# A 1-core streaming block: a written order for the recurrence on three engines, and five Strassen stages instead of two in the second down projection

## The chip, the cores and the metric

The kernel runs on one core of one Trainium2 chip. The metric is the device time of one execution in microseconds (us). Smaller is better. Five engines work beside each other and wait for one another through semaphores: TensorE (PE in the profile; its weight loads are PEld), VectorE (DVE), ScalarE (ACT), GpSimd (POOL) and SyncE (SP), which here issues the DMA transfers.

## What is computed

One block of a streaming encoder on 512 tokens of width 1024: a half-step SwiGLU FFN, a token mixer, and a second half-step FFN. Each is modulated (shift, scale, gate from the conditioning vector c). The mixer joins a gated DeltaNet group (4 heads, causal convolution, chunked delta rule) and a latent-attention group (4 heads). Cut to what matters:

```python
def _swiglu(h, w_in, w_out):
    gate, up = jnp.split(h @ w_in, 2, axis=-1)
    return (jax.nn.silu(gate) * up) @ w_out

    # chunked delta rule, one step of the scan over chunks
    def step(state, inp):
        u_c, wk_c, qd_c, kd_c, qk_c, gl_c = inp
        v_new = u_c - jnp.einsum('bhck,bhkv->bhcv', wk_c, state)
        o_c = jnp.einsum('bhck,bhkv->bhcv', qd_c, state) + jnp.einsum('bhcs,bhsv->bhcv', qk_c, v_new)
        state = state * gl_c[..., None, None] + jnp.einsum('bhck,bhcv->bhkv', kd_c, v_new)
        return state, o_c

    o_a = _rms(o_a, gdn_norm_w) * jax.nn.silu(gz.reshape(B, S, GDN_HEADS, GDN_DV))
    mixed = jnp.concatenate([o_a.reshape(B, S, GDN_WIDTH), o_b.reshape(B, S, MLA_WIDTH)], axis=-1)
    return mixed @ w_out

        x = x + 0.5 * g1[:, None, :] * _swiglu(h, ffn1_w_in[l], ffn1_w_out[l])
        x = x + g2[:, None, :] * y      # y: the mixer of the modulated x
        x = x + 0.5 * g3[:, None, :] * _swiglu(h, ffn2_w_in[l], ffn2_w_out[l])
```

The hidden width of the FFNs is 2816, which is 22 tiles of 128. All values are fp32.

## The kernel before

**Products.** The transposed activations stay on chip, 512 tokens wide (`xT`, one tile for each 128 of the 1024 channels). Every fp32 value is split in a rounded part and a rest (`wh` and `wl` of a weight `wr`, `ah` and `al` of the hidden activations, `mh` and `ml` of the mixed heads), and a product is the sum of three matmuls (`mm3`: wh·xh, wh·xl, wl·xh, lines 468 to 470). A "dense product" below is one such matmul of 128 by 128 weights on 512 columns. ScalarE makes the rounded part by a cast, VectorE the rest by a subtraction, for weights in `split_w` (lines 228 and 229) or `sevenths` (line 269 on VectorE).

**Strassen stages.** In the gate/up products and in a part of the down projections a block of two output tiles, 8 tiles of the contraction and two halves of the tokens is treated as a 2 by 2 block product and computed by seven products, each 12 matmuls of 256 columns (L354 and, in the second down projection, L1250). The seven weight combinations (`sevenths`) and the activation combinations (`act_sums`, tiles `t`, split in `th` and `tl`) are made by VectorE and ScalarE beside TensorE. `seven_down` runs one such stage; `PAIRED = (4, 6)` names the first output tile of each.

**The second down projection** (`last_down`). There are 22 tiles of the contraction, in three parts (`KPARTS`: 8, 8 and 6 tiles). Output tiles 0 to 3 are dense, all 22. For tiles 4 and 5, and for 6 and 7, the first 8 contraction tiles are a Strassen stage, the other 14 are dense. The last tile's dense part is computed in two token halves. After each output tile VectorE adds it into `xT` (`update`, L1129), and `store` transposes it on TensorE (four times 128 by 128, L1286), copies it on ScalarE (L1288) and sends 256 KB through SyncE (L136). The end of the program is the last half tile: two updates, two transposes (L1228), a copy on ScalarE and one on VectorE, and two small stores.

**The recurrence** (`recur`, `gated_out`). The 512 tokens are four blocks `p` of 128. For each block, the matmuls with the state `S` (L1966, L1974) give `vn` on VectorE (L1968), which the matmuls for the new state (L1981) and for the output (L1989) read. The output `o` of a block is then normed (`gated_out`: squares on ScalarE, their sum `gs`, `ve`, an rsqrt `ry` on GpSimd at L214, the scaled `on` at L1475), transposed on TensorE (L2012), multiplied (`mf`), and split in `mh` and `ml`. Between these small steps TensorE fills with dense products of the output projection (`out_attended`, `out_half`, `out_rest`).

**What sets the order.** A scheduler of the tile framework orders each engine's instructions by a priority list and its own cost model. The context `matmuls_in_order` around the recurrence loop takes only TensorE out of its hands: the matmuls follow each other as the code writes them, save for the `loosely` recorded ones. VectorE and ScalarE are ordered by the scheduler there. Every engine works its queue in order; SyncE's queue holds all DMA transfers. Weight buffers (`wr`, `wh`, `wl`) come four at a time, accumulators (`pa`) three.

Of the kernel before, what the change touches and what calls it, by code (L numbers as in the profile page):

```python
# [19 lines left out]
P = 128  # L20
# [11 lines left out]
PAIRED = (4, 6)  # L32
# [64 lines left out]
class Block:  # L97
# [66 lines left out]
    @contextmanager  # L164
    def matmuls_in_order(self, after=None):

        self.loose = set()
        with self.traced() as block:
            yield
        for i in block:  # L170
            if i.engine == mybir.EngineType.PE and i.name not in self.loose:
                if after:
                    self.follow(i, after)
                after = i.name
        self.last_mm = after
# [81 lines left out]
    def unit_rows(self, w, t):  # L257

        raws = [self.raw_tile() for _ in range(2)]
        for i, raw in enumerate(raws):  # L260
            self.load(raw, w[:8 * P, (t + i) * P:(t + i + 1) * P].rearrange("(k p) f -> p k f", p=P))
        return lambda: self.sevenths(*raws, tile=lambda n: self.slot(F32R, n).rearrange("p (k f) -> p k f", k=4))
# [157 lines left out]
    def plan_units(self):  # L420
# [4 lines left out]
        def ffn(w1, w2, first, ts, seven=(), paired=()):  # L425
# [6 lines left out]
            for t in ts:  # L432
                if t in paired:
                    self.specs.append(lambda t=t: self.unit_rows(w2, t))
                for k0, n in KPARTS[1 if t in paired or t - 1 in paired else 0:]:
                    self.specs.append(lambda k0=k0, n=n, t=t: self.unit(w2[k0 * P:(k0 + n) * P, t * P:(t + 1) * P], n))

        ffn(ins["ffn1_w_in"][0], ins["ffn1_w_out"][0], 3, range(KT), SEVEN[0])
# [11 lines left out]
        ffn(ins["ffn2_w_in"][0], ins["ffn2_w_out"][0], 0, range(KT), SEVEN[1], PAIRED)  # L450
# [649 lines left out]
    def act_sums(self, whole):  # L1100

        l, r = slice(0, HALF), slice(HALF, NT)
        sub = lambda out, x, y: self.nc.vector.tensor_tensor(out=out, in0=x, in1=y, op=ALU.subtract)
        self.t7 = {1: [], 2: [], 3: [], 4: []}
        for a, b in zip(whole[:4], whole[4:]):
# [13 lines left out]
    def last_down(self, act, gate):  # L1119

        nc = self.nc
        full, l, r = slice(0, NT), slice(0, HALF), slice(HALF, NT)
        last, held = KT - 1, []
        side, sums, parts7 = Side(), Side(), Side()
# [7 lines left out]
        def run(p, u, ts, part, first=0, k=0, n=None):  # L1132
            k0, m = KPARTS[part]
            for j in range(k, k + (n or m)):
                xh, xl = act[k0 + j]
                self.mm3(p[:, ts], u[0][:, j, :], u[1][:, j, :], xh[:, ts], xl[:, ts], k0 + j == first, k0 + j == FT - 1)

        p = self.acc()
        for i, (k0, n) in enumerate(KPARTS):
            u = self.next_unit()  # L1140
            for k in range(0, n, 2):
                while any(not isinstance(a, tuple) for a in act[:k0 + k + 5]):
                    self.splits.step()
                run(p, u, full, i, 0, k, 2)
        held.append((0, full, p))
        p = self.acc()
        for i in range(3):
            run(p, self.next_unit(), full, i)
            side.step(4)
        held.append((1, full, p))  # L1150

        def ahead():
            parts7.add(self.raws.pop(0)())
            parts7.step(2)

        p = self.acc()
        for i in range(3):
            u = self.next_unit()
            for k in range(0, KPARTS[i][1], 2):
                run(p, u, full, i, 0, k, 2)  # L1160
                sums.step(2)
            if i == 0:
                side.flush()
                for h in held:
                    update(*h)
            elif i == 1:
                self.store(0, range(NB))
        sums.flush()
        update(2, full, p)
        p = self.acc()  # L1170
        for i in range(3):
            u = self.next_unit(ahead=1 if i < 2 else 0)
            if i == 0:
                self.preload(2)
            elif i == 1:
                ahead()
            for k in range(0, KPARTS[i][1], 2):
                run(p, u, full, i, 0, k, 2)
                if i:
                    parts7.step()  # L1180
            if i < 2:
                self.store(1 + i, range(NB))
        parts7.flush()
        update(3, full, p)
        for t in PAIRED:
            self.preload(1)
            done = [3] if t == PAIRED[0] else [t - 1]
            stores = [lambda: self.prefetch(1), lambda: self.preload(1)] + [lambda x=x: self.store(x, range(NB)) for x in done]
            self.seven_down(self.weights7, act, t, update, iter(stores))
            if t + 1 == last:  # L1190
                break
            for e in range(2):
                p = self.acc()
                for i in (1, 2):
                    u = self.next_unit(ahead=0 if (e, i) == (1, 2) else 1)
                    if (e, i) == (0, 2):
                        self.preload(2)
                    elif (e, i) == (1, 1):
                        ahead()
                    for k in range(0, KPARTS[i][1], 2):  # L1200
                        run(p, u, full, i, 8, k, 2)
                        if e:
                            parts7.step()
                    if (e, i) == (1, 1):
                        self.store(t, range(NB))
                update(t + e, full, p)
            parts7.flush()
        p = self.acc()
        for i in (1, 2):
            run(p, self.next_unit(), full, i, 8)  # L1210
        update(last - 1, full, p)
        units = [self.next_unit(ahead=0) for _ in (1, 2)]
        p = self.acc()
        for i, u in zip((1, 2), units):
            run(p, u, l, i, 8)
            if i == 1:
                self.store(last - 1, range(NB))
        update(last, l, p[:, l])
        p = self.acc()
        for i, u in zip((1, 2), units):  # L1220
            run(p, u, r, i, 8)
            if i == 1:
                self.store(last, range(2))
        blocks = [slice(b * P, (b + 1) * P) for b in (2, 3)]
        pts = [self.aux() for _ in blocks]
        for ts, pt in zip(blocks, pts):
            update(last, ts, p[:, ts])
            nc.tensor.transpose(pt[:, :P], self.xT[last][:, ts], self.ident)  # L1228
        outs = [self.slot(s="o") for _ in blocks]
        nc.scalar.copy(outs[0][:, :P], pts[0][:, :P])  # L1230
        nc.vector.tensor_copy(outs[1][:, :P], pts[1][:, :P])
        for ts, o in zip(blocks, outs):
            self.load(self.out[0][ts, last * P:], o[:, :P])

# [1254 lines left out]
```

## Time and profile before

| | |
|---|---|
| median of 3 runs | 1026.66 us (1026.34 to 1027.6) |
| the profiled execution | 1026.66 us |
| its span | 1024.9 us |
| TensorE busy in the span | 99% |
| VectorE, ScalarE, GpSimd busy | 76%, 49%, 3% |
| granted TensorE clock | 1.00 |

The profile is one execution. The span is the time from its first instruction to its last; the execution's own time is 1.8 us longer. In a row of the timeline the columns are start, duration, engine, line, operation, output and inputs, shapes and count; the bracket at the end gives the idle time before it and what ended that. Tile numbers are left out (`wl`, `pa`).

### The profile page before, as it was taken

The numbers are of one execution on the slowest core, as the hardware profiler recorded it, in microseconds if no ns is written. First come the engines' busy times: TensorE is split into PE (matmuls) and PEld (weight loads), VectorE is DVE, ScalarE is ACT, GpSimd is POOL, SyncE is SP. The second block draws the span as 40 slices with busy tenths as digits, with TensorE's granted clock in tenths as the row PEclk, the third lists the DMA queues.
The fourth block names the chain that finished last, engine by engine and source line by source line (L and its number), as shares of the span: only waits on it lengthen the run. The fifth ranks groups of instructions, "written<-read, shape, count | busy, mean of one in ns | idle before, by whom it ended". The sixth has DMA issues, their size and how long they took to land.

```text
span 1024.9 us, 16967 instructions
## 1 busy us (share of the span) xinstructions
PE 1013.4 (99%) x6663; PEld 906.2 (88%) x6663; DVE 775.8 (76%) x1363; ACT 500.6 (49%) x895; POOL 29.4 (3%) x74
## 2 busy tenths in 40 slices
PE   8999999999999999999999999999999999999998
PEld 6788899999887899888888888998999999987887
DVE  4789788887787847879888659677888888788541
ACT  5453455556322235567845465364555555634330
POOL 0000000000100000100000011000000000000000
PEclk9999999999999999999999999999999999999999
DMA  9988234344688835311321121122233434383421
GB/s 328 291 271 263 69 98 116 91 123 114 198 290 303 262 83 167 83 42 42 73 73 47 42 83 49 34 58 87 83 108 99 117 90 123 115 274 91 130 61 31
DMA packets 203773, 130.77 MB, mean 128 GB/s; under 512 B 14241, under 2 KB 188334, under 8 KB 203694
## 3 DMA queue, kind: packets, MB, share of 16 engines
q1 hardware_dynamic: 203694, 129.70, 41.9%
q8 instruction: 52, 0.85, 0.3%
q14 instruction: 27, 0.22, 0.1%
HBM read 127.18 MB, written 2.49 MB: 127 GB/s over the span
## 4 chain that ended last, share of the span: by engine, by line
PE 92%; DVE 5%; DMA 1%; issue 1%; ACT 0%; POOL 0%; SPq 0%; DVEq 0%; POOLq 0%
PE pa L354 17%; PE pa L468 16%; PE pa L469 16%; PE pa L470 16%; PE pb L354 13%; PE pa L1250 1%; PE pb L2188 1%; PE pb L2168 1%; PE pb L1250 1%; PE pb L468 1%; PE pb L469 1%; PE pb L470 1%; DVE wl L229 1%; DMA ar<-in_w_ada 1%; PE pb L1743 1%; PE pb L666 1%
## 5 line engine op out<-in xcount | busy, mean ns | idle before, releaser
L228 ACT CAST wh<-wr 128x1024 fp32r<-128x1024 f32 (+1 forms) x93 | 93.8, 1015 | 160.2 <-PE pa L469 130.6
L269 DVE TENSOR_TENSOR wl<-wr,wh 128x1024 fp32r<-128x1024 f32 x96 | 117.3, 1222 | 54.5 <-ACT wh L273 54.5
L229 DVE TENSOR_TENSOR wl<-wr,wh 128x1024 fp32r<-128x1024 f32 (+1 forms) x93 | 108.8, 1176 | 47.2 <-ACT wh L228 46.3
L468 PE MATMUL pa<-hh,wh 128*128 128x512 f32 (+1 forms) x357 | 137.2, 384 | 0.0
L470 PE MATMUL pa<-hh,wl 128*128 128x512 f32 (+1 forms) x357 | 134.9, 378 | 0.0
L469 PE MATMUL pa<-hl,wh 128*128 128x512 f32 (+1 forms) x357 | 134.7, 377 | 0.0
L468 PE MATMUL pa<-ah,wh 128*128 128x512 f32 (+1 forms) x356 | 132.3, 372 | 0.0
L469 PE MATMUL pa<-al,wh 128*128 128x512 f32 (+1 forms) x356 | 131.1, 368 | 0.0
L470 PE MATMUL pa<-ah,wl 128*128 128x512 f32 (+1 forms) x356 | 130.9, 368 | 0.0
L273 ACT CAST wh<-wr 128x1024 fp32r<-128x1024 f32 x96 | 98.0, 1050 | 18.6 <-PE pa L469 11.2
L468 PEld LDWEIGHTS pa<-ah,wh 128*128 128x128 f32 x356 | 67.1, 188 | 13.4 <-ACT wh L228 2.5
L468 PEld LDWEIGHTS pa<-hh,wh 128*128 128x128 f32 x357 | 67.3, 189 | 13.2 <-issue 1.6
L837 DVE SCALAR_TENSOR_TENSOR aa<-ar,sc,aa 128x512 f32<-128x512 f32 x98 | 73.3, 749 | 6.8 <-DMA ar<-in_w_ada 4.8
L470 PEld LDWEIGHTS pa<-hh,wl 128*128 128x128 f32 x357 | 67.3, 188 | 11.9
L470 PEld LDWEIGHTS pa<-ah,wl 128*128 128x128 f32 x356 | 67.1, 188 | 11.0
L469 PEld LDWEIGHTS pa<-hl,wh 128*128 128x128 f32 x357 | 67.4, 189 | 10.7
L469 PEld LDWEIGHTS pa<-al,wh 128*128 128x128 f32 x356 | 67.1, 189 | 10.8
L354 PE MATMUL pa<-hh,wh 128*128 128x256 f32 x240 | 68.0, 283 | 0.0
L354 PE MATMUL pa<-th,wh 128*128 128x256 f32 x240 | 67.9, 283 | 0.0
L354 PE MATMUL pa<-tl,wh 128*128 128x256 f32 x240 | 67.9, 283 | 0.0
L354 PE MATMUL pa<-th,wl 128*128 128x256 f32 x240 | 67.9, 283 | 0.0
L354 PE MATMUL pa<-hh,wl 128*128 128x256 f32 x240 | 67.9, 283 | 0.0
(481 smaller groups left out, 2482.4 us busy)
## 6 DMA issues: line engine op xcount, KB each, us to landing
wr<-in_ffn_w_in SPq DMA_DIRECT2D x79, 512.0 KB
ar<-in_w_ada SPq DMA_DIRECT2D x96, 256.0 KB
wr<-in_ffn_w_out SPq DMA_DIRECT2D x32, 512.0 KB
ar<-in_w_ada SPq DMA_DIRECT2D x22, 512.0 KB
wr<-in_w_in SPq DMA_DIRECT2D x21, 512.0 KB
wr<-in_ffn_w_out SPq DMA_DIRECT2D x16, 384.0 KB
wr<-in_w_out SPq DMA_DIRECT2D x8, 512.0 KB
wr<-in_ffn_w_in SPq DMA_DIRECT2D x8, 384.0 KB
```

Of the source, the lines that this page charges most:

```text
L228: self.nc.scalar.copy(hi, raw)
L229: self.nc.vector.tensor_tensor(out=lo, in0=raw, in1=hi.bitcast(F32), op=ALU.subtract)
L269: sub = lambda out, x, y: nc.vector.tensor_tensor(out=out, in0=x, in1=y, op=ALU.subtract)
L273: nc.scalar.copy(hi[:, :n], raw[:, :n])
L354: nc.tensor.matmul(z, a[:, j, :], b, start=start and j == 0 and i == 0, stop=j == 3 and i == 2, skip_group_check=not start)
L468: mm(out, wh, xh, start=start, stop=False)
L469: mm(out, wh, xl, start=False, stop=False)
L470: mm(out, wl, xh, start=False, stop=stop)
L666: nc.tensor.matmul(pg[32 * q:32 * q + 32, :256], self.sc[:, kc:kc + 1].to_broadcast([P, 32]), a[kc], start=(e == 0), stop=(e == 1), tile_p ...
L837: nc.vector.scalar_tensor_tensor(out=acc, in0=a, scalar=sc, in1=acc, op0=ALU.mult, op1=ALU.add)
L1250: nc.tensor.matmul(z, a[:, j, :], b, start=start and j == 0 and i == 0, stop=j == 3 and i == 2, skip_group_check=not start)
L1743: nc.tensor.matmul(pa[:, ps], kh[:, ps], x[:, ps], start=True, stop=True)
```

## The change

**Part A, the order of the recurrence.** `steps_in_order` takes the place of `matmuls_in_order`. It makes VectorE and ScalarE follow the written order too, except for steps recorded as `loose`, and for the last block's final steps, which are `free` on these two. `gated_out` is divided in more steps, and the loop over the blocks writes out in which order the steps of one block and of its predecessor follow. The transposes of a block's output come right behind the next block's output matmuls.

**Part B, the plan of the second down projection.** A table, `PLAN`, takes the place of the code for each group of tiles. "all" is a dense tile over all 22 contraction tiles, "tail" one over the last 6 alone, "most" one over parts 0 and 2 (14 tiles). A pair of numbers (k, t) is a Strassen stage over contraction part k for the output tiles t and t+1, written S(k,t) below. There are five: S(0,4), S(0,6), S(1,2), S(1,4), S(1,6). `act_sums` runs twice, the second time on contraction tiles 8 to 15, of which only the split parts still exist; eight additions (`aw`) put the whole values together again. The last tile is no longer computed in halves. The program ends in the stage S(1,6), whose end holds the store of tile 7 and the last two blocks of tile 6.

```diff
-PAIRED = (4, 6)
+SEVENS = 0, 1
+PLAN = (("all", 0), ("all", 1), ("tail", 4), ("tail", 5), ("tail", 6), ("tail", 7), (0, 4), (0, 6), ("most", 2), ("most", 3),
+        (1, 2), (1, 4), (1, 6))
+MISSING = {"all": (), "most": (1,), "tail": (0, 1)}
...
-    def matmuls_in_order(self, after=None):
+    def steps_in_order(self):
+
+        self.loose, self.free, last = set(), set(), {}
+        engines = mybir.EngineType.PE, mybir.EngineType.DVE, mybir.EngineType.Activation
         with self.traced() as block:
             yield
         for i in block:
+            if i.engine != engines[0] and i.name in self.free:
+                continue
+            if i.engine in engines and i.name not in self.loose:
+                if i.engine in last:
+                    self.follow(i, last[i.engine])
+                last[i.engine] = i.name
...
-    def act_sums(self, whole):
+    def act_sums(self, tiles):
...
+        def whole(x):
+            if not isinstance(x, tuple):
+                return x
+            a = self.slot(s="aw")
+            tt(out=a, in0=x[0].bitcast(F32), in1=x[1].bitcast(F32), op=ALU.add)
+            return a
...
+        for at, (kind, t) in enumerate(PLAN):
+            after = [k for k, _ in PLAN[at + 1:at + 3]] + ["all"] * 2
+            if kind in SEVENS:
...
+                self.seven_down(w, act, 8 * kind, t, update, work, stores())
+                work.flush()
+                if kind:
+                    ended += [t, t + 1]
+                elif after[0] not in SEVENS:
+                    sums.add(self.act_sums(act[8:16]))
+                continue
...
         product(za, 3, False)
-        update(t, r, za)
+        if not last:
+            update(t, r, za)
+            return
+        self.store(t + 1, range(NB))
+        blocks = [slice(b * P, (b + 1) * P) for b in (2, 3)]
+        pts = [self.aux() for _ in blocks]
+        for ts, pt in zip(blocks, pts):
+            update(t, ts, za[:, ts.start - HALF:ts.stop - HALF])
+            nc.tensor.transpose(pt[:, :P], self.xT[t][:, ts], self.ident)
...
             for p in range(NB):
                 while self.wk[p] is None:
                     loosely(chain, 1)
...
+                steps = self.recur(p)
+                outs.append(self.gated_out(p))
...
+                past = outs[p - 1]
+                next(steps)
+                next(past)
+                between(3)
+                next(steps)
+                next(past)
+                next(outs[p])
+                next(past)
+                next(outs[p])
+                next(past)
+                if p == 2:
                     fill.add(half())
+                between(3)
```

The line numbers of the changed kernel differ by a few to some tens. Three places in the order of the instructions show what moves. The first is VectorE at block 3 of the recurrence, around `vn` (the row with L1968). Before:

```order
L2018 SCALAR_TENSOR_TENSOR mf_6770<-pb_6765,cwT_3625,z_6196 128x128
L2021 TENSOR_TENSOR ml_6532<-mf_6770,mh_6531 128x128
L2021 TENSOR_TENSOR ml_6534<-mf_6770,mh_6533 128x128
L2018 SCALAR_TENSOR_TENSOR mf_6770<-pb_6765,cwT_3625,z_6353 128x128
L2021 TENSOR_TENSOR ml_6536<-mf_6770,mh_6535 128x128
L2028 TENSOR_REDUCE gs_6783<-hn_6784 128x4
L2021 TENSOR_TENSOR ml_6538<-mf_6770,mh_6537 128x128
L2003 SCALAR_TENSOR_TENSOR ve_6787<-gs_6783,oe_5895 128x4
L1968 TENSOR_TENSOR vn_6797<-uu_6572,pb_6792 128x512
L2403 SCALAR_TENSOR_TENSOR xT_99<-pa_6755,mod_3430,xT_99 128x512
L1475 TENSOR_TENSOR on_6819<-o_6697,ry_6789 128x512
```

And VectorE at the same place after (`vn` is now in L1960):

```order
L1996 TENSOR_REDUCE gs_6750<-hn_6751 128x4
L1998 SCALAR_TENSOR_TENSOR ve_6763<-gs_6750,oe_5895 128x4
L2018 TENSOR_TENSOR ml_6532<-mf_6753,mh_6531 128x128
L2018 TENSOR_TENSOR ml_6534<-mf_6753,mh_6533 128x128
L2018 TENSOR_TENSOR ml_6536<-mf_6753,mh_6535 128x128
L2018 TENSOR_TENSOR ml_6538<-mf_6753,mh_6537 128x128
L1463 TENSOR_TENSOR fl_6772<-fr_6360,fh_6771 128x512
L235 TENSOR_TENSOR wl_6778<-wr_6775,wh_6777 128x1024
L1960 TENSOR_TENSOR vn_6797<-uu_6575,pb_6792 128x512
L1467 TENSOR_TENSOR on_6808<-o_6697,ry_6765 128x512
```

The four `mf`, `gs` and `ve` of the previous block now come first, then its `ml`, one `fl` and one weight split `wl`, and then `vn`.

The second place is VectorE ahead of the last `on` of the recurrence, which the last transposes on TensorE read. Before:

```order
L2018 SCALAR_TENSOR_TENSOR mf_6853<-pb_6848,cwT_3625,z_6353 128x128
L2028 TENSOR_REDUCE gs_6866<-hn_6867 128x4
L2021 TENSOR_TENSOR ml_6534<-mf_6853,mh_6533 128x128
L2021 TENSOR_TENSOR ml_6536<-mf_6853,mh_6535 128x128
L2021 TENSOR_TENSOR ml_6538<-mf_6853,mh_6537 128x128
L2003 SCALAR_TENSOR_TENSOR ve_6870<-gs_6866,oe_5895 128x4
L1471 TENSOR_TENSOR fl_6875<-fr_6364,fh_6874 128x512
L1475 TENSOR_TENSOR on_6884<-o_6791,ry_6872 128x512
```

After:

```order
L1996 TENSOR_REDUCE gs_6832<-hn_6833 128x4
L1998 SCALAR_TENSOR_TENSOR ve_6845<-gs_6832,oe_5895 128x4
L2018 TENSOR_TENSOR ml_6532<-mf_6835,mh_6531 128x128
L2018 TENSOR_TENSOR ml_6534<-mf_6835,mh_6533 128x128
L2018 TENSOR_TENSOR ml_6536<-mf_6835,mh_6535 128x128
L2018 TENSOR_TENSOR ml_6538<-mf_6835,mh_6537 128x128
L1463 TENSOR_TENSOR fl_6854<-fr_6363,fh_6853 128x512
L2417 SCALAR_TENSOR_TENSOR xT_99<-pa_6814,mod_3430,xT_99 128x512
L235 TENSOR_TENSOR wl_6867<-wr_6864,wh_6866 128x1024
L1467 TENSOR_TENSOR on_6874<-o_6791,ry_6847 128x512
```

`gs` and `ve` moved ahead of all `ml`, and an `xT` update and a `wl` stand between them and `on` that did not stand there before.

The third place is in the second down projection, on VectorE, between the weight combinations of a Strassen stage and the updates. Before, ahead of its last stage:

```order
L229 TENSOR_TENSOR wl_10678<-wr_10651,wh_10677 128x768
L269 TENSOR_TENSOR wl_10682<-wr_10653,wh_10681 128x1024
L269 TENSOR_TENSOR wr_10653<-wr_10653,wr_10654 128x512
L292 TENSOR_TENSOR wr_10654<-wr_10654 128x512
L269 TENSOR_TENSOR wr_10654<-wr_10654,wr_10653 128x512
L1129 SCALAR_TENSOR_TENSOR xT_99<-pa_10616,mod_10284,xT_99 128x512
L269 TENSOR_TENSOR wr_10653<-wr_10653,wr_10654 128x512
L269 TENSOR_TENSOR wl_10705<-wr_10654,wh_10704 128x1024
L269 TENSOR_TENSOR wl_10716<-wr_10653,wh_10715 128x1024
```

After, ahead of S(1,2) (`aw`, `t` and `tl` belong to the second set of activation combinations):

```order
L1463 TENSOR_TENSOR tl_10815<-t_10778,th_10814 128x512
L275 TENSOR_TENSOR wr_10747<-wr_10747,wr_10748 128x512
L275 TENSOR_TENSOR wl_10805<-wr_10748,wh_10804 128x1024
L1117 TENSOR_TENSOR aw_10828<-ah_9947,al_9948 128x512
L1117 TENSOR_TENSOR aw_10830<-ah_10020,al_10021 128x512
L1111 TENSOR_TENSOR t_10832<-aw_10828 128x256
L275 TENSOR_TENSOR wl_10820<-wr_10747,wh_10819 128x1024
L1111 TENSOR_TENSOR t_10832<-aw_10830,t_10832 128x256
L1111 TENSOR_TENSOR t_10833<-aw_10830,aw_10828 128x256
L1111 TENSOR_TENSOR t_10833<-aw_10830,t_10832 128x256
L1145 SCALAR_TENSOR_TENSOR xT_99<-pa_10740,mod_10242,xT_99 128x512
L1463 TENSOR_TENSOR tl_10847<-t_10832,th_10846 128x512
```

The activation combinations now stand between the weight combinations, and TensorE reads both in the stages that follow.

More of the change, by code (lines that the diff above doesn't have):

```diff
@@ L1121, in last_down @@
         nc = self.nc
-        full, l, r = slice(0, NT), slice(0, HALF), slice(HALF, NT)
-        last, held = KT - 1, []
-        side, sums, parts7 = Side(), Side(), Side()
+        full = slice(0, NT)
+        side, sums, parts7, ended, held = Side(), Side(), Side(), [], []
         side.add(self.ada_rest((3,), True))
@@ L1130, in update @@
                                            in1=self.xT[t][:, ts], op0=ALU.mult, op1=ALU.add)
[L1132 to L1150, printed above, removed]
         def ahead():
+            self.preload(1)
             parts7.add(self.raws.pop(0)())
[L1154 to L1167, printed above, removed]
@@ L1184, in last_down @@
[L1184 to L1207, printed above, removed]
@@ L1208, in last_down @@
[L1208 to L1233, printed above, removed]
```

218 lines of the change are left out of this document (131 added, 87 removed).

## The prediction

> **What bounds the kernel now.** I read the page first (busy time, then the chain that ended last), then the list of waits, then the timeline at each wait and at the end of the program.
>
> ```profile
> PE 1013.4 (99%) x6663; PEld 906.2 (88%) x6663; DVE 775.8 (76%) x1363; ACT 500.6 (49%) x895; POOL 29.4 (3%) x74
> ```
>
> ```profile
> PE pb L1989 <- DVE vn L1968: 1.1, 1, 1.1
> PE pb L2012 <- DVE on L1475: 0.9, 1, 0.9
> ```
>
> TensorE is busy 99% of the span. Time can go in two ways only: fewer TensorE steps, or less of the 11.5 us (a span of 1024.9 less 1013.4) in which it stands. The longest waits behind the first load are the two quoted, both in the recurrence, and VectorE ends both. Part A of the change (the written order) moves the rows around them; part B (five Strassen stages) changes the number of steps.
>
> **Part A, first wait.** The timeline of VectorE, then of TensorE, around it:
>
> ```profile
> 632.17 0.68 DVE L2028 TENSOR_REDUCE gs<-hn 128x4 f32<-128x512 f32 x1
> 632.77 0.28 DVE L2021 TENSOR_TENSOR ml<-mf,mh 128x128 fp32r<-128x128 f32 x1
> 632.97 0.15 DVE L2003 SCALAR_TENSOR_TENSOR ve<-gs,oe 128x4 f32<-128x4 f32 x1
> 633.04 0.68 DVE L1968 TENSOR_TENSOR vn<-uu,pb 128x512 f32<-128x512 f32 x1
> ...
> 632.26 0.39 PE L470 MATMUL pa<-mh,wl 128*128 128x512 f32 x1
> 633.78 0.94 PE L1989 MATMUL pb<-vn,qk 128*128 128x128 f32 x6 [1.12 <-DVE vn L1968]
> ```
>
> TensorE starts its last dense product at 632.26 and the next matmul, which reads vn, at 633.78: 1.52 us where a dense product of 512 columns takes 0.23 (worked out under part B), so 1.29 are lost. vn itself is 0.68 long; it stood behind work on the previous block's output (gs, ml, ve), which no matmul needed yet. In the changed order that work is issued a dense run earlier, because its transposes are; directly before vn stands the split of a weight (wl, 1.22 by its group below).
>
> The two engines can be run against each other from the end of the previous block's qk products. VectorE's order from there is o, four mf, gs, ve, four ml, fl, wl, vn: 0.69 + 4 × 0.28 + 0.68 + 0.15 + 4 × 0.28 + 0.69 + 1.22 + 0.68 = 6.4 (mf at ml's price, o and fl at that of the 512-wide rows). Rows that follow each other start 0.08 sooner than the durations say (vn started at 633.04, though ve lasted 0.15 from 632.97), 13 times 0.08 less: 5.3, and 0.2 until the first starts, 5.5. TensorE's order is 4 transposes, 18 dense products and 8 small matmuls: 12 × 0.11 (the L1286 row below) + 18 × 0.2275 = 5.4. It is a tie: of the 1.29 I take **1.2** as gone.
>
> **Part A, second wait.** The same a block later, with the rsqrt on GpSimd in the path; VectorE, then TensorE:
>
> ```profile
> 639.60 0.68 DVE L2028 TENSOR_REDUCE gs<-hn 128x4 f32<-128x512 f32 x1
> 640.19 0.69 DVE L2021 TENSOR_TENSOR ml<-mf,mh 128x128 fp32r<-128x128 f32 x3
> 640.80 0.15 DVE L2003 SCALAR_TENSOR_TENSOR ve<-gs,oe 128x4 f32<-128x4 f32 x1
> 640.87 0.69 DVE L1471 TENSOR_TENSOR fl<-fr,fh 128x512 fp32r<-128x512 f32 x1
> 642.46 0.69 DVE L1475 TENSOR_TENSOR on<-o,ry 128x512 f32<-128x512 f32 x1 [0.90 <-POOL ry L214]
> ...
> 641.87 0.39 PE L470 MATMUL pa<-mh,wl 128*128 128x512 f32 x1
> 643.21 0.66 PE L2012 MATMUL pb<-ident,on 128*128 128x128 f32 x4 [0.95 <-DVE on L1475]
> ```
>
> From 641.87 to 643.21 it is 1.34 us, 1.11 above a dense step. The chain is gs, ve, the rsqrt ry on GpSimd, on: 1.5 us pass between ve's end (640.95) and on (642.46), and in 0.90 of them VectorE idles. After the change gs and ve stand ahead of all four ml, and ry runs beside these. The same race from the start of vn: VectorE has vn, on, xT, o, four mf, gs, ve, four ml, fl, xT, wl and the last on, which add up to 9.2 (eight 128-wide rows at 0.28, xT at 0.75 and wl at 1.22 from the groups below, the others from these rows), less 17 × 0.08: 7.9, with vn's own 0.6 included. TensorE, which starts when vn ends, has 8 small matmuls and 30 dense products: 7.7, so it asks 0.4 after on is there. **1.1** gone.
>
> Together part A is worth **−2.3** us. Its bounds: −2.9, if smaller waits of a few tenths in this region close too, and −1.1, if one of the two only changes its place. No matmul is removed, so it can give no more than such gaps.
>
> **Part B, the products.** The chain that ended last, around one Strassen stage and the dense run ahead of it:
>
> ```profile
> 957.25 0.23 PE pa L468
> ...
> 959.98 1.43 PE pa L1250 x12
> 961.41 1.44 PE pb L1250 x12
> ...
> 967.17 0.44 PE pb L1286 x4
> ```
>
> Twelve dense products start between 957.25 and 959.98: 0.2275 each. Twelve Strassen products of 256 columns take 1.44: 0.120 each, 5% more per column. Both run without gaps. Counted from the code, the second down projection issues 390 dense, 168 Strassen and 84 half-tile (256 wide) products now, afterwards 288 dense and 5 × 84 = 420 Strassen. So 102 × 0.2275 = 23.2 us go and (420 − 252) × 0.120 = 20.2 come: **−3.0 us**. A stage saves 48 × 0.2275 − 84 × 0.120 = 0.84, and three more make 2.5; the rest is the last tile, which is no longer computed in halves.
>
> The Trainium skill, page "TensorE: Matmul & The Clock Gate", section "Back-to-back issue gap", gives an isolated gap of N/2.4 GHz plus about 2.5 ns: 215.8 ns for 512 columns and 109.2 for 256. By it these terms would be −3.7 instead of −3.0. The rows are slower at both widths, and the sum goes by the rows.
>
> **Part B, what VectorE must do beside it.** VectorE's groups from 900 us on:
>
> ```profile
> L229 DVE TENSOR_TENSOR wl<-wr,wh 128x1024 fp32r<-128x1024 f32 x9 | 11.0, 1224 | 6.8 <-ACT wh L228 6.7
> ...
> L1471 DVE TENSOR_TENSOR tl<-t,th 128x512 fp32r<-128x512 f32 x8 | 5.3, 685 | 0.5 <-ACT th L1470 0.5
> L1129 DVE SCALAR_TENSOR_TENSOR xT<-pa,mod,xT 128x512 f32<-128x512 f32 x7 | 5.2, 748 | 12.8 <-PE pa L470 12.8
> ...
> L1103 DVE TENSOR_TENSOR t<-af,t 128x256 f32<-128x256 f32 x8 | 3.4, 421 | 0.1
> ```
>
> And windows, the first from a gate/up stretch made of Strassen stages alone, the other two from the second down projection (TensorE's busy time comes first, VectorE's third):
>
> ```profile
> 750.00:800.00 50.00, 50.00 (x419) 50.00 (x418) 41.94 (x60) 27.77 (x50) 0.00 (x0) 1.00 0.37 105
> ...
> 900.00:950.00 50.00, 50.00 (x226) 40.23 (x225) 40.45 (x65) 18.53 (x28) 0.00 (x0) 1.00 0.54 177
> 950.00:1000.00 50.00, 50.00 (x308) 44.89 (x307) 26.63 (x36) 18.42 (x27) 0.00 (x0) 1.00 0.34 98
> ```
>
> The second set of sums costs 8 aw adds and 8 tl at 0.685 (aw is the same width from two inputs) and 16 t at 0.42: 17.7 us. Each of three more stages costs 3 wl of 1.22, sl and four combinations at 0.685 instead of two wl of 1.22: 4.6 more, 14 in all. So some 32 us join the 67 (40.45 + 26.63) of these 100 us: nearly full, but hidden on average. The cover is TensorE's own work, as in the gate/up window, where 41.94 of 50 leave TensorE full.
>
> The tightest place lies between most2 and the interleaved stages S(1,2) and S(1,4) (names of the plan, see the section on the change). By the order, 46 VectorE instructions stand there from S(0,6)'s 512-wide update to the wl of S(1,4)'s first product. Their durations add up to 29.6 us (3 updates of 0.75, 3 half ones at 0.42 like t, 5 wl of 1.22 and a three-quarter one of 0.92, 7 tl, 6 aw and 5 combinations at 0.685, 16 t at 0.42). Less 0.08 for each, as above, it is 26. TensorE reaches that wl 27 us after the start: 4 of S(0,6), 84 × 0.2275 = 19.1 of most2 and most3, and 27 × 0.120 of what follows, with tenths of turns. So the wait is between 0 and 2.5 us. I take 0.25, near the lower end because the rows do start sooner, and 0.2 at the second tail tile, whose accumulator tile 0's update must set free. **+0.45** (0 to 2.5).
>
> **Part B, the tail.** Now TensorE's last two steps and SyncE's last issues:
>
> ```profile
> 1020.49 0.28 PE L470 MATMUL pa<-ah,wl 128*128 128x256 f32 x1
> ...
> 1021.21 0.65 PE L1228 MATMUL pb<-ident,xT 128*128 128x128 f32 x2 [0.45 <-DVE xT L1129]
> ...
> 1021.91 0.82 SPq L136 DMA_DIRECT2D out_x<-o  x2
> ```
>
> Afterwards four transposes of tile 7 stand between these two steps. The same four (0.44, the L1286 row above) stood ahead of the last products; where they go, TensorE waits for xT anyway (0.72 from 1020.49 to 1021.21): **−0.44**. In return ScalarE copies 512 columns before its last small copy, and SyncE issues three DMAs instead of two: +0.41, half of 0.82. The 256 KB of tile 7 may also still move when the small ones start; at 0.8 us (the highest rate of a slice on the page is 328 GB/s) that is up to 0.8 more. **+0.8** (0.4 to 1.2).
>
> **Sum.** −2.3 − 3.0 + 0.45 − 0.44 + 0.8 = −4.5. The span becomes 1020.4. The profiled execution took 1026.66 with its 1024.9 of span (1.8 around it) and is also the median of three runs (1026.34 to 1027.6), so the forecast is **1022.2**.
>
> **Rivals.** (1) *The wait in the recurrence only changes its place.* ScalarE and VectorE follow a written order too: if the transfer or the cast of the split ahead of vn is late, vn waits behind it. For it: both races end within tenths. Against it: ScalarE is busy 49% of the span, so the cast can go ahead early. One wait kept gives back 1.1 or 1.2, 1023.4; both 1024.5.
>
> (2) *VectorE becomes the bound in the second down projection, and the kernel gets slower.* Each of the eight new tl waits for a th, which ScalarE casts from the t before it. Now the handoffs are covered (0.5 us over 8 in the tl row). In the tight stretch no other work may be left to put between; each then costs a cast and two turns, about the 0.7 of the 512-wide rows: 8 × 0.7 = 5.6, so 1027.8; with a late wl (1.22) on top 1029.0. From 4.5 us on, when VectorE's string is over 31.5 instead of 26, the kernel is slower than before. Against it: the gate/up stretch runs at 84% of VectorE without a gap. For it: here it is 96%.
>
> (3) *The stages gain nothing net.* Waits at their borders (a z buffer, a late weight part, a store in SyncE's queue) take the 2.5 us upper bound, and the tail 1.2. Then 1024.5 to 1025 is left. For it: 0.84 per stage is small, and in the gate/up window the weight loads are busy 50.00 of 50 (the second figure), so nothing there absorbs a hiccup.
>
> **How the numbers follow.** A measurement of this kernel tells about 0.2%, 2 us, from no change, so same is 1024.6 to 1028.7. The bounds of the terms together give 1020.7 to 1025.8 (−5.9 to −0.8); the upper part is the ground of rivals 1 and 3, so the forecast proper, up to 1024.0, gets 0.68, rival 1 0.11, rival 3 0.12, rival 2 0.09. Faster: 0.68, 0.10 of rival 1 and 0.02 of rival 3, 0.80. Slower: the part of rival 2 with a late wl, 0.06. Same: the rest, 0.14. The range takes in rivals 1 and 3 and reaches 0.8 below the bounds for gaps I left out: 1019.9 to 1025.9.
>
> **What the changed profile would show.** Right: among the waits no successor of L1968 or L1475 with over 0.4 us; stages of 7 × 1.44 with no gap between; a last SyncE row with three issues behind the last transposes. Wrong: TensorE idle at the first product that reads a wl or tl of S(0,4), S(1,2) or S(1,4), or behind the tail tiles; vn still late, now behind the wl.

## The result and the profile after

The changed kernel takes 1021.41 us (median of 6 runs, 1021.17 to 1021.75), the kernel before, measured with it, 1026.7 (1026.34 to 1027.6). The ratio is 0.9947, with a 95% interval of 0.9936 to 0.9957. The span of the profiled execution is 1020.0 us, 4.9 less than before; the medians are 5.3 apart. A second load of the same changed kernel took 1021.66 (ratio 0.9953, 0.9941 to 0.9966).

The page's busy times of the changed kernel, then its list of waits on TensorE:

```profile
PE 1010.3 (99%) x6729; PEld 908.1 (89%) x6729; DVE 809.1 (79%) x1428; ACT 513.5 (50%) x921; POOL 28.9 (3%) x74
```

```profile
PE pb L526 <- DMA xt<-in_x: 4.7, 1, 4.7
PE pb L541 <- DMA vecs<-in_b_ada: 0.5, 1, 0.5
PE pb L2039 <- DVE qrT L2099: 0.4, 1, 0.4
```

Both waits of the recurrence are gone from the list, and no new one has come. VectorE's work grew by 33 us (809.1 against 775.8), as the 32 of the sum said. The timeline of VectorE around the vn of block 3 and the last `on`, then of TensorE where it reads them:

```profile
629.49 0.68 DVE L1463 TENSOR_TENSOR fl<-fr,fh 128x512 fp32r<-128x512 f32 x1
630.09 1.22 DVE L235 TENSOR_TENSOR wl<-wr,wh 128x1024 fp32r<-128x1024 f32 x1
631.23 0.68 DVE L1960 TENSOR_TENSOR vn<-uu,pb 128x512 f32<-128x512 f32 x1
...
638.10 1.21 DVE L235 TENSOR_TENSOR wl<-wr,wh 128x1024 fp32r<-128x1024 f32 x1
639.23 0.68 DVE L1467 TENSOR_TENSOR on<-o,ry 128x512 f32<-128x512 f32 x1
...
632.20 0.40 PE L477 MATMUL pa<-mh,wl 128*128 128x512 f32 x1
632.44 1.05 PE L1981 MATMUL pb<-vn,qk 128*128 128x128 f32 x8
...
640.37 0.40 PE L477 MATMUL pa<-mh,wl 128*128 128x512 f32 x1
640.61 0.60 PE L2007 MATMUL pb<-ident,on 128*128 128x128 f32 x4
```

vn ends at 631.91, TensorE takes it at 632.44, one dense step after the product before it. `on` ends at 639.91 and is taken at 640.61. The cushions are 0.5 and 0.7 us.

To compare kernels this close, I measure distances inside each trace, between rows that all of them have. Three distances cover the change: from the last transposes of the attention output ahead of the recurrence (reading `on`, L2210 before, L2208 after) to the first matmul of the conditioning (reading `aa` and `ones`, L859 or L866), which holds all of part A; from there to the last product; and from the last product to the end of the span. In the runs below, parts that an edit does not touch repeat them within 0.03 us (the tail within 0.07). The rows of the changed kernel that they start from and end at, on TensorE:

```profile
608.82 0.63 PE L2208 MATMUL pb<-ident,on 128*128 128x128 f32 x4
...
924.08 1.05 PE L866 MATMUL pb<-aa,ones 128*32 128x512 f32 x4
...
1014.99 0.28 PE L1228 MATMUL pa<-ah,wl 128*128 128x256 f32 x1
```

The distances, before and after:

| us | mixer to conditioning | conditioning to last product | last product to end |
|---|---|---|---|
| before | 318.08 | 93.75 | 4.41 |
| changed | 315.26 | 90.91 | 5.01 |
| difference | −2.82 | −2.84 | +0.60 |

Together they make −5.06; 0.16 of it went to the start, where TensorE waits for the first loads.

### The profile page after: what moved, and what is told of

The parts are those of the page before. It is cut to its first block, busy times and chain, and to the rows that moved or that the text cites. A ratio compares the mean times of both kernels' runs of the same rounds, so it can differ in the third digit from the quotient of the medians.

```text
span 1020.0 us, 17205 instructions
## 1 busy us (share of the span) xinstructions
PE 1010.3 (99%) x6729; PEld 908.1 (89%) x6729; DVE 809.1 (79%) x1428; ACT 513.5 (50%) x921; POOL 28.9 (3%) x74
## 4 chain that ended last, share of the span: by engine, by line
PE 95%; DVE 3%; DMA 1%; issue 0%; ACT 0%; SPq 0%; POOL 0%; DVEq 0%
PE pa L360 17%; PE pa L475 16%; PE pa L476 15%; PE pa L477 15%; PE pb L360 13%; PE pa L1228 3%; PE pb L1228 2%; PE pb L2186 1%; PE pb L2166 1%; PE pb L475 1%; PE pb L476 1%; PE pb L477 1%; PE pb L1735 1%; PE pb L673 1%; DMA vecs<-in_b_ada 1%; DVE cv L1679 1%
## 5 line engine op out<-in xcount | busy, mean ns | idle before, releaser
L275 DVE TENSOR_TENSOR wl<-wr,wh 128x1024 fp32r<-128x1024 f32 x105 | 128.2, 1222 | 45.1 <-ACT wh L279 45.0
L234 ACT CAST wh<-wr 128x1024 fp32r<-128x1024 f32 (+1 forms) x87 | 87.3, 1012 | 146.5 <-PE pa L476 121.3
L235 DVE TENSOR_TENSOR wl<-wr,wh 128x1024 fp32r<-128x1024 f32 (+1 forms) x87 | 101.5, 1172 | 41.3 <-ACT wh L234 41.1
L279 ACT CAST wh<-wr 128x1024 fp32r<-128x1024 f32 x105 | 107.4, 1052 | 13.0 <-DVE wr L275 7.2
L475 PE MATMUL pa<-ah,wh 128*128 128x512 f32 (+1 forms) x294 | 110.5, 376 | 0.0
L476 PE MATMUL pa<-al,wh 128*128 128x512 f32 (+1 forms) x294 | 110.1, 374 | 0.0
L477 PE MATMUL pa<-ah,wl 128*128 128x512 f32 (+1 forms) x294 | 109.7, 373 | 0.0
L275 DVE TENSOR_TENSOR wr<-wr,wr 128x512 f32<-128x512 f32 x105 | 72.5, 690 | 2.0
L360 PE MATMUL pa<-hl,wh 128*128 128x256 f32 x240 | 67.9, 283 | 0.0
L475 PEld LDWEIGHTS pa<-ah,wh 128*128 128x128 f32 x294 | 55.3, 188 | 12.2 <-ACT wh L234 2.5
```

Of the source, the lines that this page charges most:

```text
L234: self.nc.scalar.copy(hi, raw)
L235: self.nc.vector.tensor_tensor(out=lo, in0=raw, in1=hi.bitcast(F32), op=ALU.subtract)
L275: sub = lambda out, x, y: nc.vector.tensor_tensor(out=out, in0=x, in1=y, op=ALU.subtract)
L279: nc.scalar.copy(hi[:, :n], raw[:, :n])
L360: nc.tensor.matmul(z, a[:, j, :], b, start=start and j == 0 and i == 0, stop=j == 3 and i == 2, skip_group_check=not start)
L475: mm(out, wh, xh, start=start, stop=False)
```

## The experiments

**The two parts alone.** e1_order has only part A of the diff (its first line below, the loop over the blocks and `gated_out`), e2_stages only part B (`PLAN` and what it drives).

```diff
-        with self.matmuls_in_order():
+        with self.steps_in_order():
```

> Part A alone (the written order of the recurrence; the second down projection as before). If the two parts are independent and part A is what closes the two waits of the recurrence (the trace after shows TensorE 2.8 us earlier at the end of the mixer, the sum of 1.29, 1.11 and some tenths), the kernel takes 1023.8 to 1024.0 us and no wait of TensorE on vn or on the scaled output is over 0.2 us. Rival: the gain of the whole change depends on both (later transfers shift into the next stage), then this run lies more than 0.5 us off that.

> Part B alone (five Strassen stages, the matmuls of the recurrence as before). Independent parts: the last product comes 2.8 us earlier than before and the tail behind it is 0.6 longer, so 2.2 us less than before, 1024.4 to 1024.6, with both waits of the recurrence (1.3 and 1.1) still there. If the stages gained only because VectorE started them less loaded behind part A, less than 1.5 us is gained.

e1_order took 1024.04 us, ratio 0.9973 (0.9962 to 0.9984). e2_stages took 1024.43, ratio 0.9979 (0.9970 to 0.9988). In the traces the three distances are 315.25, 93.75 and 4.42 for e1_order, 318.06, 90.90 and 4.95 for e2_stages: each part moves its own distance, by the whole amount, and none of the other's. In e2_stages both waits stand as before:

```profile
PE pb L1978 <- DVE vn L1957: 1.1, 1, 1.1
PE pb L2001 <- DVE on L1464: 1.0, 1, 1.0
```

**Only the matmuls in order.** e3_pe_only leaves VectorE and ScalarE to the scheduler. It ran twice.

```diff
-        engines = mybir.EngineType.PE, mybir.EngineType.DVE, mybir.EngineType.Activation
+        engines = mybir.EngineType.PE,
```

> The changed kernel, but only the matmuls follow the written order; VectorE and ScalarE are left to the scheduler. Theory 1 (what counts is where the transposes and the small steps stand in TensorE's order, VectorE follows by itself): at most 0.3 us over the changed kernel, 1021.4 to 1021.7. Theory 2 (VectorE's written order is what closes the waits): one or both waits come back, 1022.6 to 1023.9, with TensorE waiting 1 us or more at vn or at the last scaled output.

> The changed kernel once more, beside the next runs. If the time of one load of a program is the same as that of another, 1021.2 to 1021.7. If the first 100 us (where TensorE waits for the first transfers, by up to 1 us more or less in the traces so far, with the same instructions) differ from load to load, it may lie up to 1 us off, and then only distances inside a trace, from the end of the start-up on, compare kernels this close.

> The kernel of e3_pe_only once more. By its trace TensorE loses 0.63 us at vn of block 3 against the changed kernel, and it started 0.9 us later for reasons before the recurrence. If that start is a matter of the load, this run is 0.4 to 0.9 us over r_after; if it belongs to the kernel, 1.2 to 1.6.

The first load took 1022.70 (1022.53 to 1023.33), the second 1021.99 (1021.49 to 1023.93), beside r_after's 1021.66 (0.33 more, a little less than the 0.4 to 0.9 expected). But both traces have the same distances: 315.99 and 316.01 for the mixer, 0.74 over the changed kernel, and 90.90 and 90.92 behind it. What differs is the start: the row that begins the first distance stands at 609.70 and at 607.83, with the same instructions ahead of it. So the written order of VectorE and ScalarE is worth 0.74 of part A's 2.82, and the rest of part A, with the matmuls' order and the finer steps, the other 2.08. Neither theory held as stated. Where the 0.74 goes is to be seen on VectorE and GpSimd in e3_pe_only, around block 2's vn:

```profile
623.95 0.68 DVE L1960 TENSOR_TENSOR vn<-uu,pb 128x512 f32<-128x512 f32 x1
624.93 1.52 DVE L1467 TENSOR_TENSOR on<-o,ry 128x512 f32<-128x512 f32 x1 [0.30 <-POOL ry L220]
...
628.24 0.67 DVE L1985 TENSOR_TENSOR o<-o,pb 128x512 f32<-128x512 f32 x1
628.84 1.21 DVE L235 TENSOR_TENSOR wl<-wr,wh 128x1024 fp32r<-128x1024 f32 x1
...
624.88 1.04 POOL L1467 TENSOR_TENSOR Sg<-S,gl 128x512 f32<-128x512 f32 x1
```

Here ve comes later, `on` waits for ry, and then it takes 1.52 us instead of 0.68: GpSimd works on `Sg` beside it. VectorE runs late from there, and TensorE waits at vn of block 3:

```profile
633.05 0.39 PE L477 MATMUL pa<-mh,wl 128*128 128x512 f32 x1
633.81 0.38 PE L1981 MATMUL pb<-vn,qk 128*128 128x128 f32 x1 [0.37 <-DVE vn L1960]
```

In the changed kernel `Sg` runs from 621.68 to 622.72, beside two xT updates that read an accumulator, and none of the four `on` is longer than usual (2.7 us for four, against 3.6 in both loads of e3_pe_only). No run moved `Sg` alone, so this path is read from the rows and not shown by an edit.

**The transposes late.** e7_late keeps the three-engine order, but puts the transposes (and mf, ml) behind the next nine dense products.

```diff
                 next(steps)
-                next(past)
                 next(outs[p])
-                next(past)
                 next(outs[p])
-                next(past)
+                between(3)
+                next(past)
+                next(past)
+                next(past)
                 if p == 2:
                     fill.add(half())
-                between(3)
```

> The changed kernel, its three-engine order kept, but the transposes of a block's output put behind the next nine dense products again, as before the change, with mf and ml behind them and ahead of the next vn. If the early transposes are what closes the first wait, TensorE waits at vn by 1 us or more again (1022.5 to 1024). If it is enough that gs and ve (0.83 us) and the last wl no longer stand between mf and vn: mf, ml and vn take 2.6 us against TensorE's 2.9 of 8 small and 9 dense matmuls, so at most 0.3 us is lost.

1023.29 us, ratio 0.9970 (0.9959 to 0.9982); the mixer's distance is 316.91, 1.65 over the changed kernel. TensorE waits at vn (L1981), 0.5 us by the list of waits, and once more, 0.3, where an accumulator is set free late:

```profile
PE pb L1981 <- DVE vn L1960: 0.5, 1, 0.5
...
PE pa L475 <- DVE xT L2417: 0.3, 1, 0.3
```

So with the three-engine order kept, the early place of the transposes (and of the mf and ml that follow them) is worth 1.65 of the 2.82. This and the 0.74 of e3_pe_only are each measured against the changed kernel; they are not two parts of one sum. My count of mf, ml and vn against TensorE's steps left out what VectorE still has to do ahead of mf in that order:

```profile
627.16 0.69 DVE L1996 TENSOR_REDUCE gs<-hn 128x4 f32<-128x512 f32 x1 [0.76 <-ACT hn L1994]
...
628.62 1.23 DVE L235 TENSOR_TENSOR wl<-wr,wh 128x1024 fp32r<-128x1024 f32 x1
629.76 1.12 DVE L2013 SCALAR_TENSOR_TENSOR mf<-pb,cwT,z 128x128 f32<-128x128 f32 x4
630.80 0.89 DVE L2018 TENSOR_TENSOR ml<-mf,mh 128x128 fp32r<-128x128 f32 x4
631.60 0.68 DVE L1960 TENSOR_TENSOR vn<-uu,pb 128x512 f32<-128x512 f32 x1
```

gs waits 0.76 for the squares (in the changed order mf fill that time), then come fl and wl, and vn ends at 632.28, 0.6 after TensorE was free for it (its last dense product starts at 631.45).

**Four stages instead of five.** e4_four computes tiles 2 and 3 densely and drops S(1,2).

```diff
-... (0, 4), (0, 6), ("most", 2), ("most", 3),
-        (1, 2), (1, 4), (1, 6))
+... (0, 4), (0, 6), ("all", 2), ("all", 3),
+        (1, 4), (1, 6))
```

> The changed kernel with four Strassen stages: output tiles 2 and 3 are dense over all 22 tiles, S(1,2) is left out. One stage is worth 48 x 0.2275 - 84 x 0.120 = 0.84 us less the few tenths that its crowded VectorE costs (0.1 to 0.4 in the trace after): by that the run takes 1021.9 to 1022.3. Rival: at five stages VectorE is so full that the fifth gains nothing; then 1021.2 to 1021.6.

1021.35 us (1020.96 to 1022.04), ratio 0.9946 (0.9932 to 0.9959), not to be told from the changed kernel. The trace tells more: 91.20 from the conditioning to the last product, against 90.91. The fifth stage is worth 0.29 us, not 0.84. The other 0.55 are short waits inside the stages of the changed kernel. One is here, where steps of 0.12 become 0.19 and 0.22:

```profile
986.51 0.28 PE L1228 MATMUL pa<-al,wh 128*128 128x256 f32 x1
986.63 0.28 PE L1228 MATMUL pb<-ah,wh 128*128 128x256 f32 x1
986.82 0.39 PE L1228 MATMUL pa<-ah,wl 128*128 128x256 f32 x1
987.04 0.28 PE L1228 MATMUL pa<-ah,wh 128*128 128x256 f32 x1
```

The matmul at 986.82 reads the wl of S(1,4) that VectorE ended at 986.76: the end of the tight string, met 0.07 us late; with the slower step behind it 0.18 is lost. The others are steps that start at 961.72, 988.96 and 1002.18 and lose 0.1, 0.25 and 0.2. There TensorE's next weight load waits for ScalarE, which still copies the accumulator into `z` (L1240, L1248). Most of the last one (0.16) stands in e4_four too. So only a part of the 0.55 is VectorE's.

**VectorE's string made longer.** e5_twice makes each of the eight aw additions twice.

```diff
-            tt(out=a, in0=x[0].bitcast(F32), in1=x[1].bitcast(F32), op=ALU.add)
+            for _ in range(2):
+                tt(out=a, in0=x[0].bitcast(F32), in1=x[1].bitcast(F32), op=ALU.add)
```

> The changed kernel with each of the eight aw additions of the second activation sums made twice, 8 x 0.6 us = 4.8 us more of VectorE's time between most2 and S(1,4). The string theory (VectorE has no time left there: in the trace after it idles 0.6 us from 960 to 987 while TensorE waits 0.08 at the end): TensorE waits 3.5 to 4.8 us at the first products that read late wl or tl, and the run takes 1025 to 1026.2. Rival (the scheduler puts the sums earlier or finds other matmuls to run ahead): under 1.5 us more.

1026.47 us, ratio to the kernel before 0.9999 (0.9990 to 1.0008), 0.3 above the range expected. The distance from the conditioning to the last product is 95.73, 4.82 over the changed kernel, with 4.8 us of additions. The list of waits names the places, and the windows (TensorE's busy time first, the granted clock after GpSimd's column) show what followed:

```profile
PE pa L1229 <- DVE wl L275: 1.4, 1, 1.4
PE pb L1229 <- DVE wl L275: 1.3, 1, 1.3
...
PE pb L1229 <- ACT th L1463: 0.6, 1, 0.6
```

```profile
985.00:989.00 4.00, 2.09 (x14) 1.48 (x12) 4.00 (x9) 1.77 (x4) 0.00 (x0) 1.00 0.43 131
989.00:991.50 2.50, 1.24 (x10) 1.24 (x11) 2.50 (x5) 0.26 (x1) 0.00 (x0) 1.00 0.30 90
991.50:995.00 3.50, 3.50 (x19) 3.50 (x19) 2.55 (x5) 0.75 (x2) 0.00 (x0) 0.52 0.00 0
```

VectorE is busy throughout the first two windows, TensorE in half of them. Then, from 991.5 on, TensorE has work and goes at a granted clock of 0.52, with 0.21 us a step instead of 0.12. So of the 4.8, some 3.5 are the waits and 1.3 the clock (14 steps at 0.093 more): about three quarters of VectorE's extra time arrive as waits. The expectation had the waits and left out the clock.

**The additions on GpSimd.** e8_pool moves aw to the engine that is idle there.

```diff
-            tt(out=a, in0=x[0].bitcast(F32), in1=x[1].bitcast(F32), op=ALU.add)
+            self.nc.gpsimd.tensor_tensor(out=a, in0=x[0].bitcast(F32), in1=x[1].bitcast(F32), op=ALU.add)
```

> The changed kernel with the eight aw additions on GpSimd instead of VectorE, 4.8 us less for VectorE's string. If the 0.5 us that the fifth stage loses comes from VectorE's full string, TensorE's waits from 980 to 1003 (0.7 us in all in the trace after) fall below 0.3, and the distance from the row of the conditioning products (L866) to the last transposes falls from 91.9 to 91.4 to 91.6 us. Rival: GpSimd is slower at 512-wide additions and holds up the t sums behind it; then the distance is the same or longer.

1027.62 us, ratio 1.0011 (1.0002 to 1.0020): 0.1% over the kernel before. The distance is 97.18, 6.27 over the changed kernel. The eight additions take 1.68 us each on GpSimd, and VectorE beside them:

```profile
960.41 0.41 DVE L1111 TENSOR_TENSOR t<-aw,t 128x256 f32<-128x256 f32 x1
960.75 1.77 DVE L1145 SCALAR_TENSOR_TENSOR xT<-z,mod,xT 128x512 f32<-128x512 f32 x1
962.45 1.49 DVE L1111 TENSOR_TENSOR t<-aw,t 128x256 f32<-128x256 f32 x1
...
959.55 7.25 POOL L1117 TENSOR_TENSOR aw<-ah,al 128x512 f32<-128x512 f32 x4 [5.13 <-PE pa L1228]
```

The xT update takes 1.77 instead of 0.75, the t 1.49 instead of 0.42, about 1.0 longer each. By VectorE's groups from 955 us on, the wl, tl, t and xT rows lose 6.9 us in this way, more than the 5.1 of busy time that moved. The Trainium skill, page "SBUF — State Buffer", section "SBUF: two separate sides", describes a pair of SBUF ports that VectorE and GpSimd share, locked for a whole instruction, also by a VectorE operation with two SBUF inputs against a GpSimd one that reads SBUF. The trace agrees: the rows that became longer read two SBUF tiles, and so did `on` in e3_pe_only. Not every GpSimd row does this: beside the small ry (128x4, 1.12 us in the changed kernel) fl took its usual 0.68.

TensorE meets this as three waits for accumulators that ScalarE copies into `z`, 4.6 us in all:

```profile
PE pb L1228 <- ACT z L1243: 2.1, 1, 2.1
PE pa L1228 <- ACT z L1232: 1.3, 1, 1.3
PE pa L1228 <- ACT z L1248: 1.2, 1, 1.2
```

At the longest one, the cast ahead of the copy in ScalarE's row had itself waited 3.1 us for a `wr` of VectorE. Behind it the granted clock falls as in e5_twice (0.70 in the mean from 995 to 1000): 15 steps take 0.094 longer, 1.4 us.

**The tail.** e6_tail exchanges the last two products, so that two blocks of tile 7 end the program; e9_both has this and e8_pool's edit. e10_two lets ScalarE's queue issue one of the two last small stores.

```diff
-        for ts, o in zip(blocks, outs):
-            self.load(self.out[0][ts, t * P:(t + 1) * P], o[:, :P])
+        for ts, o, eng in zip(blocks, outs, (nc.scalar, nc.sync)):
+            eng.dma_start(out=self.out[0][ts, t * P:(t + 1) * P], in_=o[:, :P])
```

> The changed kernel with the last two products of the last stage exchanged, so that the program ends with two blocks of tile 7, and the last 256 KB store becomes two of 128 KB that the end does not hold all of: store of tile 6 blocks 2 and 3, tile 7 blocks 2 and 3, then two small ones. If the tail's 0.6 us is the third DMA and the 512-wide copy ahead of the small ones, the tail stays at about 5.0 us from the last product to the end of the span, or is a little longer, because four issues stand there now; a shorter one (4.4 to 4.7) only if the two stores are done beside the last products.

> Both edits, e6_tail and e8_pool, in one kernel. If they do not touch each other, the sum of their two differences to the changed kernel in the trace, within 0.2 us.

> The changed kernel with the first of its two last small stores issued by ScalarE's queue instead of SyncE's, beside the 256 KB one. If the tail's 0.6 us is the third issue in a row on SyncE (three take 1.42 in the trace after, 0.47 each), the end of the span comes 0.3 to 0.5 us nearer to the last product: 5.0 now, 4.5 to 4.7 then. If it is the 256 KB still moving, 4.9 to 5.1. Either way the median differs from the changed kernel's by less than two loads of the same kernel have differed (0.7).

e6_tail: 1021.79, a tail of 5.12 instead of 5.01, and the last product 0.25 later (in the exchanged order the step at 1012.79 loses 0.27): no gain. Four issues stand there now, 1.92 us in SyncE's row instead of 1.42. e9_both: 1027.52; 97.40 to the last product is e8_pool's 97.18 and most of e6_tail's 0.25. e10_two: 1021.94 (1021.18 to 1022.39), 90.91 and a tail of 5.05. Nothing is gained, though one issue less stands in SyncE's row. The changed kernel's three issues:

```profile
1016.35 1.42 SPq L139 DMA_DIRECT2D out_x<-o  x3
```

The third starts 2.38 us behind the start of the last product; before, the last one started 1.86 behind it. From that issue's start to the last moved byte it is 1.24 us, and 1.23 before. So in the changed kernel the later issue by itself accounts for the longer tail. In e10_two the last issue starts 1.83 behind the last product, but the last byte moves only 0.05 us sooner (3.57 behind the last product instead of 3.62): the 384 KB now move at about 340 GB/s without a break, where the two small stores of the kernel before leave gaps. The row of issues and the bytes thus end at nearly the same time, and taking away one of the two gains nothing. The end also comes 1.52 us behind the last byte in e10_two instead of 1.34; why is open. Fewer bytes were not tried.

## Why the prediction was right

The prediction said 1022.2, with 1019.9 to 1025.9; 1021.41 was measured. Its sum was −4.5 for the span; −4.9 came.

**Part A: −2.3 forecast, −2.82 measured** (the mixer's distance, the same in e1_order). Both waits closed, and VectorE won both races. I had called the first a tie, and it was won by 0.5 us. The larger of the mis-sized terms there is TensorE's. These are its rows ahead of vn in the changed kernel:

```profile
628.57 1.05 PE L1958 MATMUL pb<-S,w 128*128 128x128 f32 x8
629.46 1.06 PE L1966 MATMUL pb<-S,cv 128*128 128x128 f32 x8
630.27 0.47 PE L475 MATMUL pa<-mh,wh 128*128 128x512 f32 x1
```

I counted the 8 small fp32 matmuls with the state at 0.11 each, but each of them leaves two records (4 in the code are x8 in a row), and the two groups take 1.70 us, not 0.9. In all, TensorE needs 6.4 us from the transposes (626.04) to the products that read vn, not 5.4, and VectorE 5.9 from there to the end of vn, not 5.5. In the second race both sums were short as well: from the start of vn, `on` ends after 8.7 us, not 7.9, and TensorE asks for it after 9.4, not 8.3. That the differences still came out on the right side is in part luck, as both errors point the same way.

The rest of part A's gain over the forecast is the gaps of a few tenths that I had left out of the sum and that closed as well (at block 2's vn, and the slower matmul behind each wait); the bound of −2.9 had them. That the gain comes from the place of the transposes and from the written order together is what e7_late (1.65 lost) and e3_pe_only (0.74 lost) show.

**The products: −3.0, the waits: +0.45, the four transposes: −0.44; −2.99 forecast, −2.84 measured** (in e2_stages too). The products and transposes are counted from rows, so the waits came to about 0.6, a little above what I took. Only one of them is where the prediction put it: 0.18 at S(1,4)'s first wl, for which I had 0.25. The 0.2 at the second tail tile did not come; no step of TensorE between 927 and 945 is over its usual length by more than 0.03. In their place stand the three short waits for ScalarE's copies of accumulators (0.1, 0.25 and 0.2, under e4_four), for which the sum had no term. So the size of this term is partly luck. Rival 3 had named such a place, a z buffer.

**VectorE's string.** I had 26 us for it against TensorE's 27, and took 0.25 of wait all the same. Its first and last rows in the changed kernel:

```profile
959.67 0.74 DVE L1145 SCALAR_TENSOR_TENSOR xT<-z,mod,xT 128x512 f32<-128x512 f32 x1
...
985.54 1.22 DVE L275 TENSOR_TENSOR wl<-wr,wh 128x1024 fp32r<-128x1024 f32 x1
```

From 959.67 to 986.76 it is 27.1 us, 1.1 more than I had, of which 0.54 are two waits for ScalarE's casts (0.28 ahead of a tl, 0.26 ahead of a wl). TensorE's 27 was right. So the string has no slack, and e5_twice shows it: of 4.8 us more, some 3.5 arrive as waits.

**The tail: +0.8 forecast, +0.60 measured.** But its reason was half wrong. I added half for a third DMA issue and half for the 256 KB in motion. The rows of the tail show that the two run beside each other and end within 0.05 us, so they do not add.

Of the rivals, the first (the wait changes its place) did not come: the split ahead of vn was cast in time. It has its shape in e3_pe_only and e7_late. The second (VectorE becomes the bound, slower than before) lies close: with 4.8 us more of VectorE's time, e5_twice is level with the kernel before, near the point of 4.5 us that the prediction gave, and e8_pool is past it. What made it dear was not the handoffs between t, th and tl that I had priced (they cost 0.3 once in the trace after) but work on VectorE itself (or, in e8_pool, rows held up by GpSimd), and a clock that falls once TensorE has waited. The third (the stages gain nothing) is refuted for the plan as a whole, and nearly true for the fifth stage: 0.29.

## What to carry to other kernels

Where one engine is full, run the two order lists against each other from a common point, with start-to-start times from the rows, and look at how many records each matmul leaves in the trace. One more Strassen stage is worth what TensorE saves less what the helper engines can no longer hide; here the fifth brought a third of its count. Compare kernels that differ by less than a microsecond by distances inside their traces, not by their totals.

## What the runs showed of the hardware

- Beside a 128x512 operation on GpSimd (1.0 to 2.4 us) a VectorE instruction with two SBUF inputs took 0.8 to 1.1 us longer (0.42 became 1.49, 0.75 became 1.77, 0.68 became 1.52). Moving 5 us of work from a full VectorE to an idle GpSimd cost 6.3 us, 1.4 of it by the clock.
- In e5_twice, after some 6 us in which TensorE worked only half of the time, its granted clock fell to 0.52 for about 3 us, though no single wait was longer than 1.4 us by the list. In e8_pool it fell behind a wait of 2.1 us. The Trainium skill, page "TensorE: Matmul & The Clock Gate", section "Part 1: The HAM clock gate (the "warmup" mystery)", names an idle window of about 3.4 us behind which the clock halves. The halving agrees; here it came without an idle window of that length.
- Two runs of the same program (e3_pe_only and r_pe_only) reached the same point ahead of the recurrence at 609.70 and at 607.83, with the same instructions before it. All of the difference is there by 30 us, in rows where TensorE waits for the first transfers (xt, vecs, ar). So the start moves by up to 2 us from load to load.
